# Two layers of a hybrid encoder on one core: a sixth load buffer, copies of the norms split over two engines, and block-sum steps moved inside the matmul pairs

## The chip, the core and the metric

The kernel runs on one core of a Trainium2 chip. Five engines work side by side, each through its own queue in order: TensorE (PE, matmuls into PSUM; its weight loads are shown as PEld), VectorE (DVE), ScalarE (ACT), GpSimd (POOL) and SyncE (SP, which issues the transfers here). They wait for each other through semaphores. The metric is the device time of one execution in microseconds (us); lower is better.

## The reference, cut to what matters

The input is 256 tokens of 2048 features in float32. There are two layers. Each does `x = x + mixer(rmsnorm(x))` and then `x = x + swiglu(rmsnorm(x))`; the mixer is grouped attention in layer 0 and a gated recurrent block in layer 1. The change concerns the feed-forward half and the norms that feed it and the next mixer:

```python
def rms_norm(x, g):
    y = xf * lax.rsqrt(jnp.mean(xf * xf, axis=-1, keepdims=True) + EPS)
    return (y * g.astype(jnp.float32)).astype(x.dtype)

def swiglu(h, w_gate, w_up, w_down):        # D = 2048, D_FF = 5632
    return (jax.nn.silu(h @ w_gate) * (h @ w_up)) @ w_down

for i in range(DEPTH):                      # DEPTH = 2
    ...
    x = x + mix
    x = x + swiglu(rms_norm(x, norm_ffn[i]), w_gate[i], w_up[i], w_down[i])
```

## The kernel before, in words

**Precision.** Every weight and activation is split into a rounded part "hi" and a remainder "lo". A product is three matmuls (hi·hi, hi·lo, lo·hi) into one float32 accumulator of 512 columns.

**Loads.** Weights come as halves of 512 KB, 128 x 1024 numbers. `load_half` issues one transfer from SP's queue into a `raw` buffer (L111), casts it on ScalarE into `hi` (L120) and subtracts on VectorE into `lo` (L121). There are five `raw`, five `hi` and five `lo` buffers, used in turn. So a transfer waits until the half five places earlier was cast and subtracted, and a cast waits until TensorE is done with the half five places earlier. The order of the halves (`order`, `ffn_order`) is written out by hand and must be the order in which TensorE uses them.

**Pairs.** The feed-forward part goes in parts of 12, 16 and 16 hidden tiles (`PARTS`). For each four hidden tiles a "unit" multiplies the normalised tokens with 512 columns of w_gate and of w_up at the same time; this is one call of `project_pair`, with eight steps over the 16 feature tiles. After a part's units, `down` multiplies the part's hidden tiles with w_down in two such pairs (columns 0-1 and 2-3 of four), with six steps in the part of 12 and eight in the parts of 16. A pair has four accumulators, `banks[j][a]` with j the half of the columns and a the half of the tokens, in the four PSUM buffers of `new_acc`. The next pair uses the same four, in the order [0][0], [0][1], [1][0], [1][1], and its first products wait until VectorE has taken the old contents out.

**Steps.** A usual step takes two halves and eight products (24 matmuls, L275). In two steps of each pair, those named in `SEVEN`, a block scheme does the same with seven products (21 matmuls). It needs sums of the weight blocks: VectorE makes `wx` with four additions once both halves have landed (L245 to L248; L246 also rewrites the second `raw` before its cast), ScalarE casts `wxh` (L252), and VectorE subtracts `wxl` (L253). The fifth to seventh product read them; the first four do not. The sums of the token blocks are made by `x_forms`. The partial results go to four more PSUM banks, and once the second such step is done `merge` puts them together: a copy on ScalarE (L311) that can start after the step's first product, and four additions on VectorE (L312 to L315). Then VectorE adds the accumulators: in a unit onto gate and up (L755, L758), in `down` first four additions of the merged results onto the residual stream `x_tok` (L489), then the four accumulators (L498).

**After a unit** come SiLU on ScalarE (L515), the product with up (L759), and `turned`: two 32 x 32 transposes on VectorE (L440) into a single buffer `tb`, and 16 copies of 32 x 256 on ScalarE (L445) into a single buffer `tf`, then the hi and lo of four hidden tiles (L764, L765).

**Norms.** `Norm.add` is called for each 512 columns of `x_tok` that are final: two squares on ScalarE (L404), `turned`, and the hi and lo of four feature tiles (L396, L397). So the last columns of a mixer are turned while the first pair of the feed-forward part is running. The recurrent block begins with `project_two`, which uses the first eight feature tiles for two outputs, then four more, then the last four.

**Who sets the order.** TensorE's order is the order of the program. On the other engines a scheduler orders the instructions when the program is built, from its own estimate of times; on the chip each engine keeps that order.

Of the kernel before, what the change touches and what calls it, by code (L numbers as in the profile page):

```python
# [12 lines left out]
F32 = mybir.dt.float32  # L13
# [5 lines left out]
P = 128  # L19
S = 256  # L20
D = 2048
KT = D // P
# [4 lines left out]
DFF = 5632  # L27
PARTS = [12, 16, 16]
SEVEN = {6: (1, 3), 8: (2, 5)}
HALF = 8  # L30
WIDE = 512
NCOL = D // WIDE
FOUR = WIDE // P
# [37 lines left out]
def trunk(ctx, tc, w, out):  # L71
    nc = tc.nc
    act, dve, pool, pe, sync = nc.scalar, nc.vector, nc.gpsimd, nc.tensor, nc.sync

    cst = ctx.enter_context(tc.tile_pool(name="cst", bufs=1))
    wp = ctx.enter_context(tc.tile_pool(name="wp", bufs=3))
# [10 lines left out]
    def nm(s):  # L87
        uid[0] += 1
        return f"{s}_{uid[0]}"
# [15 lines left out]


    def load_half(src, n, pieces=1, then=None, before=None):
        raw = wp.tile([P, HALF, P], F32, tag="raw", name=nm("raw"), bufs=5)
        hi = wp.tile([P, HALF, P], F32R, tag="hi", name=nm("hi"), bufs=5)
        lo = wp.tile([P, HALF, P], F32R, tag="lo", name=nm("lo"), bufs=5)  # L110
        newest["load"] = sync.dma_start(out=raw[:, :n, :], in_=src[:, :n, :])  # L111
        newest["raw"] = raw
        if then:
            then()
        if before:
            before(raw)
        for i in range(pieces):
            sl = slice(i * n // pieces, (i + 1) * n // pieces)
            newest["tiles"] = hi, lo
            newest["cast"] = act.copy(hi[:, sl, :], raw[:, sl, :])  # L120
            dve.tensor_tensor(lo[:, sl, :], raw[:, sl, :], hi[:, sl, :].bitcast(F32), ALU.subtract)  # L121
        return [(hi[:, i, :], lo[:, i, :]) for i in range(n)]


    def halves(src, kt):
        return [(src[:, a : min(a + HALF, kt), :], min(HALF, kt - a)) for a in range(0, kt, HALF)]

    def wide(name):
        src = w[name]
        return [(src[c, i], HALF) for c in range(src.shape[0]) for i in range(src.shape[1])]  # L130

    def ffn_order(l):
        units = [wide(f"w_gate{l}"), wide(f"w_up{l}")]
        seq, i = [], 0
        for p, n in enumerate(PARTS):
            for _ in range(n // FOUR):
                seq += sum(zip(*(u[i : i + KT // 2] for u in units)), ())
                i += KT // 2
            down = wide(f"w_down{l}_{p}")
            for c in range(0, len(down), n):  # L140
                seq += sum(zip(down[c : c + n // 2], down[c + n // 2 : c + n]), ())
        return seq

    order = [(w["w_k"][i], HALF) for i in range(len(KEY_TILES))]
    order += sum((halves(w["w_qv"][h % 20], KT) for h in range(NQ, NQ + 20)), [])
    order += wide("w_o") + ffn_order(0)
    for b in range(-1, NBLK):
        xin = range(2 * b + 2, 2 * b + 4) if b + 1 < NBLK else []
        yin = range(KT + 2 * b, KT + 2 * b + 2) if b >= 0 else []
        both = [halves(w["w_in"][c], KT) for c in (*xin, *yin)]  # L150
# [35 lines left out]
    def step():  # L186
        clock[0] += 1
        due = [i for i, (t, _) in enumerate(waiting) if t <= clock[0]]
        if due:
            waiting.pop(due[0])[1]()  # L190
# [5 lines left out]
    def new_acc():  # L196
        return ps_a.tile([P, 2 * S], F32, tag="acc", name=nm("acc"))
# [37 lines left out]
    def flat(t):  # L235
        return t.rearrange("p (k c) f -> p k (c f)", k=2)
# [29 lines left out]
        dve.tensor_tensor(t[:, 1], y[:, 4:, :], t[:, 0].bitcast(F32), ALU.subtract)  # L266
        return [(t[:, 0, i, :], t[:, 1, i, :]) for i in range(4)]

    def project_pair(xs, forms, middle):
        banks = [[new_acc() for _ in range(2)] for _ in range(2)]  # L270
        begun = set()

        def product(acc, x, wt, last=False):
            for i, (a, b) in enumerate(((x[0], wt[0]), (x[0], wt[1]), (x[1], wt[0]))):
                pe.matmul(acc, a, b, start=id(acc) not in begun, stop=last and i == 2)  # L275
                begun.add(id(acc))
            step()
            step()

        def tokens(k, a):  # L280
            return [xs[k][:, o + a * P : o + (a + 1) * P] for o in (0, S)]

        end = len(xs) // 2 - 1
        for n in range(end + 1):
            if n in forms:
                s1, s2, s3, s4 = forms[n]
                b11, b21, t3, b22, t1, t2, t4 = seven_forms()
                if n == min(forms):
                    p1, q6, q5, q7 = (ps_m.tile([P, WIDE], F32, tag="pm", name=nm("pm")) for _ in range(4))
                last = n == max(forms)  # L290
                product(p1, tokens(2 * n, 0), b11, last)
                product(banks[0][0], tokens(2 * n + 1, 0), b21)
                product(banks[1][0], s4, b22)
                product(q7, s3, t3, last)
                product(q5, s1, t1, last)
                product(q6, s2, t2, last)
                product(banks[0][1], tokens(2 * n + 1, 1), t4)
                if last:
                    middle(p1, q5, q6, q7)
            else:  # L300
                for j in range(2):
                    half()
                    hi, lo = (flat(t) for t in newest["tiles"])
                    for a in range(2):
                        for k in range(2):
                            product(banks[j][a], tokens(2 * n + k, a), (hi[:, k, :], lo[:, k, :]), n == end and k == 1)
        return banks

    def merge(p1, q5, q6, q7):
        g, u = (fp[0].tile([P, 2, WIDE], F32, tag=t, name=nm(t), bufs=1) for t in ("fg", "fu"))  # L310
        act.copy(g[:, 0, :], p1)  # L311
        dve.tensor_tensor(g[:, 1, :], q6, g[:, 0, :], ALU.subtract)  # L312
        dve.tensor_tensor(u[:, 0, :], q5, g[:, 1, :], ALU.add)
        dve.tensor_tensor(g[:, 1, :], q7, g[:, 1, :], ALU.subtract)
        dve.tensor_tensor(u[:, 1, :], u[:, 0, :], q7, ALU.subtract)  # L315
        return g, u
# [66 lines left out]
    class Norm:  # L383
# [18 lines left out]
        def add(self, c):  # L402
            for a in range(2):
                act.activation(tmp("nj", (P, WIDE), bufs=1), x_tok[:, a, c, :], AF.Square, accum_out=self.sums[:, a, c : c + 1])  # L404
            for f in turned(x_tok[:, :, c, :]):
                self.operand(f, True)
            for n in SEVEN[KT // 2] if self.seven else ():
                if FOUR * c <= 2 * n < FOUR * c + FOUR:
# [24 lines left out]

    def turned(src):
        b = fp[0].tile([P, 2, FOUR, P], F32, tag="tb", name=nm("tb"))
        f = fp[0].tile([P, 8, FOUR, 32], F32, tag="tf", name=nm("tf"))
        for a in range(2):
            dve.transpose(b[:, a, :, :], src[:, a, :])  # L440
        for q in range(4):
            for i in range(4):
                o, y = f[32 * i : 32 * i + 32, q::4, :, :], b[32 * q : 32 * q + 32, :, i, :]
                y = y.rearrange("p a (k t) -> p a k t", k=FOUR)
                act.copy(o, y)  # L445
        return [f[:, :, k, :] for k in range(FOUR)]

    fp = []
# [65 lines left out]
    def table_act(*a, **k):  # L514
        table_op(act.activation(*a, **k))  # L515
# [194 lines left out]
    def act_tile():  # L710
        return xp.tile([P, 2 * S], F32R, tag="act", name=nm("act"), bufs=18)
# [35 lines left out]


    def ffn(norm, nxt):
        def unit(hid, forms, seven):  # L750
            got = []
            banks = project_pair(norm.xs, norm.forms, lambda *banks: got.extend(merge(*banks)))
            g, u = got
            for a, acc in enumerate(banks[0]):
                dve.tensor_tensor(g[:, a, :], acc, g[:, a, :], ALU.add)  # L755
                table_act(g[:, a, :], g[:, a, :], AF.Silu, scale=norm.rt[:, a : a + 1])
            for a, acc in enumerate(banks[1]):
                dve.tensor_tensor(u[:, a, :], acc, u[:, a, :], ALU.add)  # L758
                dve.scalar_tensor_tensor(u[:, a, :], u[:, a, :], norm.rt[:, a : a + 1], g[:, a, :], ALU.mult, ALU.mult)  # L759
            first = len(hid)  # L760
            for f in turned(u):
                h = act_tile()
                hi, lo = (h[:, o : o + S].rearrange("p (q t) -> p q t", t=32) for o in (0, S))
                act.copy(hi, f)  # L764
                dve.tensor_tensor(lo, f, hi.bitcast(F32), ALU.subtract)  # L765
                hid.append(h)
            for i, n in enumerate(seven):
                if first <= 2 * n < len(hid):
                    forms[n] = x_forms(hid[2 * n], hid[2 * n + 1], f"hf{i}")

        for p, n in enumerate(PARTS):
            hid, forms = [], {}
            for _ in range(n // FOUR):
                unit(hid, forms, SEVEN[n // 2])
            last = p == len(PARTS) - 1
            if last and nxt is not None:
                ln_exp_tables()
            down(hid, forms, nxt if last else None, last and nxt is None)
# [106 lines left out]
    units = [(d, j) for j in range(2) for d in range(2)]  # L885
# [114 lines left out]
```

## Time and profile before

| | |
|---|---|
| time, median of three runs | 2037.86 us (2032.6 to 2040.56) |
| profiled execution: its time, and the span on the core | 2037.47 us, 2035.7 us |
| TensorE busy | 1996.2 us, 98% |
| VectorE busy | 1692.5 us, 83% |
| ScalarE busy | 1369.3 us, 67% |
| GpSimd busy | 168.7 us, 8% |
| granted TensorE clock, mean | 0.992 |
| traffic | 386 MB, 190 GB/s; 57% of the transfer engines' span |

A row of a timeline gives the start and the duration in us, then engine, line, operation, and `out<-in` by the names of tiles; an `x4` merges four like instructions; the bracket at the end is the idle time before it and what ended it. The matmuls are pipelined: each is shown with 0.39 us though one starts every 0.227 us, so starts are compared and not durations. On VectorE and ScalarE, too, one instruction starts shortly before the row of the last one ends. A row of the windows view gives the borders of a stretch and its length, then busy time and number of instructions of PE, PEld, DVE, ACT and POOL, then the granted clock, the share of the transfer engines, and GB/s.

### The profile page before, as it was taken

The numbers are of one execution on the slowest core, as the hardware profiler recorded it, in microseconds if no ns is written. First come the engines' busy times: TensorE is split into PE (matmuls) and PEld (weight loads), VectorE is DVE, ScalarE is ACT, GpSimd is POOL, SyncE is SP. The second block draws the span as 40 slices with busy tenths as digits, with TensorE's granted clock in tenths as the row PEclk, the third lists the DMA queues.
The fourth block names the chain that finished last, engine by engine and source line by source line (L and its number), as shares of the span: only waits on it lengthen the run. The fifth ranks groups of instructions, "written<-read, shape, count | busy, mean of one in ns | idle before, by whom it ended". The sixth has DMA issues, their size and how long they took to land.

```text
span 2035.7 us, 27908 instructions
## 1 busy us (share of the span) xinstructions
PE 1996.2 (98%) x9920; PEld 1689.5 (83%) x9920; DVE 1692.5 (83%) x2351; ACT 1369.3 (67%) x2166; POOL 168.7 (8%) x213
## 2 busy tenths in 40 slices
PE   9999999999999999999799999999999999999999
PEld 8898878878888888887699998878788878888887
DVE  8998678987888888888679887688897888878887
ACT  7665876664667446677789988767745766457663
POOL 1563000000000000000133330000000000000000
PEclk9999999999999999999899999999999999999999
DMA  8444555556555665655456554656556556655564
GB/s 320 156 135 145 194 180 194 188 191 196 191 201 183 222 197 189 205 184 196 155 172 187 184 176 158 207 167 205 186 188 195 188 199 213 196 193 187 199 217 145
DMA packets 109003, 386.06 MB, mean 190 GB/s; under 512 B 12224, under 2 KB 12992, under 8 KB 108736
## 3 DMA queue, kind: packets, MB, share of 16 engines
q1 hardware_dynamic: 108720, 384.26, 57.1%
q8 instruction: 78, 1.28, 0.2%
q14 instruction: 61, 0.50, 0.1%
q10 hardware_dynamic: 144, 0.02, 0.0%
HBM read 382.13 MB, written 2.10 MB: 189 GB/s over the span
## 4 chain that ended last, share of the span: by engine, by line
PE 47%; issue 42%; DVE 7%; DMA 2%; ACT 2%; POOL 0%; SPq 0%; DVEq 0%; ACTq 0%; POOLq 0%
PE acc L275 23%; PE acc L228 4%; PE acc L206 4%; PE pm L275 3%; DVE lo L121 3%; PE acc L319 3%; PE acc L320 3%; PE acc L321 3%; PE pm L320 1%; PE pm L321 1%; PE pm L319 1%; DMA raw<-in_w_up_dram 1%; ACT tf L445 1%; ACT hi L120 1%; DMA raw<-in_w_down_dram 0%
## 5 line engine op out<-in xcount | busy, mean ns | idle before, releaser
L120 ACT CAST hi<-raw 128x1024 fp32r<-128x1024 f32 (+1 forms) x708 | 727.6, 1045 | 477.6 <-PE acc L275 372.1
L121 DVE TENSOR_TENSOR lo<-raw,hi 128x1024 fp32r<-128x1024 f32 (+1 forms) x708 | 852.4, 1223 | 135.3 <-ACT hi L120 133.9
L275 PE MATMUL acc<-hi,xg 128*128 128x512 f32 x2200 | 697.7, 390 | 3.0 <-DVE fg L755 2.9
L275 PEld LDWEIGHTS acc<-hi,xg 128*128 128x128 f32 x2200 | 413.8, 188 | 95.5 <-issue 6.4
L275 PE MATMUL acc<-lo,xg 128*128 128x512 f32 x1100 | 428.6, 390 | 0.0
L275 PE MATMUL acc<-hi,act 128*128 128x512 f32 x1072 | 342.6, 391 | 0.9 <-DVE fg L755 0.7
L275 PEld LDWEIGHTS acc<-lo,xg 128*128 128x128 f32 x1100 | 207.0, 188 | 42.3
L275 PEld LDWEIGHTS acc<-hi,act 128*128 128x128 f32 x1072 | 201.9, 188 | 48.4 <-issue 3.0
L445 ACT COPY tf<-tb 32x256 f32<-32x256 f32 x544 | 219.5, 404 | 9.2 <-DVE xg L397 1.0
L275 PE MATMUL acc<-lo,act 128*128 128x512 f32 x536 | 209.2, 390 | 0.0
L228 PE MATMUL acc<-hi,act 128*128 128x512 f32 x512 | 159.9, 390 | 0.0
L319 PE MATMUL acc<-xg,hi 128*128 128x256 f32 x512 | 147.0, 287 | 11.7 <-ACT xg L396 11.7
L320 PE MATMUL acc<-xg,hi 128*128 128x256 f32 x512 | 146.6, 286 | 0.5 <-DVE xg L397 0.5
L245 DVE TENSOR_TENSOR wx<-raw,raw 128x512 f32<-128x512 f32 x68 | 47.0, 691 | 119.7 <-DMA raw<-in_w_up_dram 91.5
L321 PE MATMUL acc<-xg,lo 128*128 128x256 f32 x512 | 146.0, 285 | 0.0
L253 DVE TENSOR_TENSOR wxl<-wx,wxh 128x1536 fp32r<-128x1536 f32 x68 | 119.1, 1752 | 22.4 <-ACT wxh L252 22.1
L206 PE MATMUL acc<-xg,hi 128*128 128x512 f32 x384 | 125.7, 396 | 0.2 <-ACT hi L120 0.2
L252 ACT CAST wxh<-wx 128x1536 fp32r<-128x1536 f32 x68 | 100.3, 1476 | 34.5 <-DVE wx L248 34.5
L275 PEld LDWEIGHTS acc<-lo,act 128*128 128x128 f32 x536 | 100.9, 188 | 20.4
L228 PEld LDWEIGHTS acc<-hi,act 128*128 128x128 f32 x512 | 96.1, 188 | 19.6
L319 PEld LDWEIGHTS acc<-xg,hi 128*128 128x128 f32 x512 | 99.8, 195 | 12.1 <-ACT xg L396 12.1
L320 PEld LDWEIGHTS acc<-xg,hi 128*128 128x128 f32 x512 | 99.7, 195 | 1.1 <-DVE xg L397 1.0
(238 smaller groups left out, 2830.4 us busy)
## 6 DMA issues: line engine op xcount, KB each, us to landing
raw<-in_w_gate_dram SPq DMA_DIRECT2D x176, 512.0 KB, 4.4
raw<-in_w_up_dram SPq DMA_DIRECT2D x176, 512.0 KB, 4.3
raw<-in_w_down_dram SPq DMA_DIRECT2D x176, 512.0 KB, 4.3
raw<-in_w_in_dram SPq DMA_DIRECT2D x64, 512.0 KB, 4.5
raw<-in_w_qv_dram SPq DMA_DIRECT2D x40, 512.0 KB, 4.3
raw<-in_w_o_dram SPq DMA_DIRECT2D x32, 512.0 KB, 3.6
raw<-in_w_out_dram SPq DMA_DIRECT2D x32, 512.0 KB, 4.3
graw<-in_w_gates_dram SPq DMA_DIRECT2D x32, 256.0 KB, 3.5
```

Source lines behind the costliest of these rows:

```text
L120: newest["cast"] = act.copy(hi[:, sl, :], raw[:, sl, :])
L121: dve.tensor_tensor(lo[:, sl, :], raw[:, sl, :], hi[:, sl, :].bitcast(F32), ALU.subtract)
L206: pe.matmul(o, w, x, start=(k == 0 and not part), stop=(k == total - 1 and not part))
L228: pe.matmul(accs[a], x, wt[:, k, :], start=(k0 + k == 0 and n == 0), stop=(end and k == 1 and n == 2))
L245: dve.tensor_tensor(x[:, 0, :], r2[:, 0, :], r1[:, 0, :], ALU.add)
L252: act.copy(xh, x)
L253: dve.tensor_tensor(xl, x, xh[:].bitcast(F32), ALU.subtract)
L275: pe.matmul(acc, a, b, start=id(acc) not in begun, stop=last and i == 2)
L319: pe.matmul(o, hi, x[:, :S], start=start, stop=False)
L320: pe.matmul(o, hi, x[:, S:], start=False, stop=False)
L321: pe.matmul(o, lo, x[:, :S], start=False, stop=stop)
L445: act.copy(o, y)
```

## The change

Three edits. `raw` has six buffers in place of five. In the norms (not in the units) every second of the 16 copies of `turned` goes to VectorE. And the steps of a pair are taken in a listed order: in the first pair of each layer's feed-forward part 0, 1, 3, 4, 2, 6, 5, 7, so that the block-sum steps (2 and 5) come fifth and seventh and no longer third and sixth; in the pairs of six 0, 2, 1, 4, 3, 5, so that the block-sum steps (1 and 3) come third and fifth and no longer second and fourth. Other pairs of eight stay as they are. The halves are loaded in the new order.

```diff
+USUAL_STEPS = {6: (0, 2, 1, 4, 3, 5), 8: (0, 1, 2, 3, 4, 5, 6, 7)}
+FIRST_STEPS = (0, 1, 3, 4, 2, 6, 5, 7)
...
-        raw = wp.tile([P, HALF, P], F32, tag="raw", name=nm("raw"), bufs=5)
+        raw = wp.tile([P, HALF, P], F32, tag="raw", name=nm("raw"), bufs=6)
...
+    def pair_steps(n, first=False):
+        return FIRST_STEPS if first else USUAL_STEPS[n]
...
             for _ in range(n // FOUR):
-                seq += sum(zip(*(u[i : i + KT // 2] for u in units)), ())
+                for k in pair_steps(KT // 2, i == 0):
+                    seq += [u[i + k] for u in units]
                 i += KT // 2
             down = wide(f"w_down{l}_{p}")
             for c in range(0, len(down), n):
-                seq += sum(zip(down[c : c + n // 2], down[c + n // 2 : c + n]), ())
+                for k in pair_steps(n // 2):
+                    seq += [down[c + k], down[c + n // 2 + k]]
...
-        end = len(xs) // 2 - 1
-        for n in range(end + 1):
+        steps = pair_steps(len(xs) // 2, first)
+        seven = [n for n in steps if n in forms]
+        for n in steps:
             if n in forms:
...
-                if n == min(forms):
+                if n == seven[0]:
...
-                last = n == max(forms)
+                last = n == seven[-1]
...
-                            product(banks[j][a], tokens(2 * n + k, a), (hi[:, k, :], lo[:, k, :]), n == end and k == 1)
+                            product(banks[j][a], tokens(2 * n + k, a), (hi[:, k, :], lo[:, k, :]), n == steps[-1] and k == 1)
...
-    def turned(src):
+    def turned(src, both=True):
...
-                act.copy(o, y)
+                if i % 2 and both:
+                    dve.tensor_copy(o, y)
+                else:
+                    act.copy(o, y)
...
-            for f in turned(u):
+            for f in turned(u, False):
...
-            for _ in range(n // FOUR):
-                unit(hid, forms, SEVEN[n // 2])
+            for i in range(n // FOUR):
+                unit(hid, forms, SEVEN[n // 2], p == i == 0)
```

More of the change, by code (lines that the diff above doesn't have):

```diff
@@ L267, in x_forms, with project_pair @@
         return [(t[:, 0, i, :], t[:, 1, i, :]) for i in range(4)]
-    def project_pair(xs, forms, middle):
+    def project_pair(xs, forms, middle, first=False):
         banks = [[new_acc() for _ in range(2)] for _ in range(2)]
@@ L749, in ffn, with unit @@
     def ffn(norm, nxt):
-        def unit(hid, forms, seven):
+        def unit(hid, forms, seven, first):
             got = []
-            banks = project_pair(norm.xs, norm.forms, lambda *banks: got.extend(merge(*banks)))
+            banks = project_pair(norm.xs, norm.forms, lambda *banks: got.extend(merge(*banks)), first)
             g, u = got
```

## The prediction, made before the changed kernel was run

> **What bounds the kernel now.** I read the page first, then the waits, the windows of single pairs, and the timelines around each stop.
>
> ```profile
> PE 1996.2 (98%) x9920; PEld 1689.5 (83%) x9920; DVE 1692.5 (83%) x2351; ACT 1369.3 (67%) x2166; POOL 168.7 (8%) x213
> ```
>
> TensorE is the bound, so the change can win only what TensorE stands still or runs slowly, and lose by making it stop elsewhere. The waits view names who stops whom (total, times, longest):
>
> ```profile
> PE pm L275 <- ACT wxh L252: 6.3, 4, 2.0
> PE pm L275 <- DVE wxl L253: 6.2, 5, 1.3
> PE acc L275 <- DVE fg L755: 3.6, 6, 1.4
> ACT hi L120 <- PE acc L275: 372.1, 210, 5.0
> DVE wx L245 <- DMA raw<-in_w_up_dram: 91.5, 37, 4.0
> ```
>
> The first two rows are the weight sums of a few block-sum steps that come late. The windows, cut where a pair's first matmul starts, say which (layer 0: first pair, first and second down pair of six, an undisturbed pair of eight; layer 1: first pair, first down pair of six):
>
> ```profile
> 267.45:314.54 47.09, 44.59 (x187) 35.89 (x186) 38.18 (x52) 31.20 (x48) 0.00 (x0) 0.96 0.57 190
> 399.63:436.40 36.77, 33.56 (x139) 26.83 (x138) 31.68 (x41) 23.18 (x37) 0.00 (x0) 0.95 0.53 171
> 436.40:468.14 31.74, 31.73 (x139) 25.75 (x138) 31.02 (x37) 15.58 (x15) 0.00 (x0) 1.00 0.65 215
> 468.14:510.30 42.16, 42.16 (x187) 34.91 (x186) 32.03 (x36) 20.68 (x21) 0.00 (x0) 1.00 0.60 188
> 1318.74:1365.81 47.07, 44.58 (x188) 35.91 (x186) 38.51 (x52) 31.21 (x48) 0.00 (x0) 0.96 0.57 191
> 1451.19:1489.62 38.43, 35.02 (x139) 27.81 (x139) 31.96 (x41) 23.43 (x37) 0.00 (x0) 0.91 0.51 164
> ```
>
> A matmul every 0.227 us gives 5.44 us for a usual step (24) and 4.76 for a block-sum step (21): 42.16 for eight steps, 31.28 for six. So each first pair loses 4.9 us, the first down pair of six 5.0 and 6.7, the second only 0.5. VectorE is busy 31.0 of 31.74 us in the second: it has no slack there. One such stop, on TensorE:
>
> ```profile
> 418.00 0.39 PE L275 MATMUL pm<-hi,hf 128*128 128x512 f32 x1
> 420.31 0.50 PE L275 MATMUL pm<-wxh,hf 128*128 128x512 f32 x1 [1.91 <-ACT wxh L252]
> 422.10 0.79 PE L275 MATMUL pm<-wxl,hf 128*128 128x512 f32 x1 [1.29 <-DVE wxl L253]
> ...
> 424.40 0.63 PE L275 MATMUL acc<-wxh,act 128*128 128x512 f32 x1
> 424.82 0.62 PE L275 MATMUL acc<-wxl,act 128*128 128x512 f32 x1
> 425.75 0.39 PE L275 MATMUL acc<-lo,act 128*128 128x512 f32 x1
> ```
>
> From 418.00 to 425.75 eleven matmuls start, which need 2.50 us: 5.25 lost, 3.20 of it idle, 2.05 at half pace (424.40 to 424.82 is 0.42). A stop costs its idle time and some 2.05 us more.
>
> **Part A, first pairs (block-sum steps fifth and seventh): -5.0 us.** The late `wxh` stands on ScalarE behind the 16 copies of the norm's last columns. At the fifth place it is wanted 10.9 us later (two usual steps), and the copies ahead of it are halved; the 2 x 4.9 us go. What is late next: `merge` now has one step before the pair ends instead of two. Call E the end of the last block-sum step; TensorE wants the second accumulator emptied at E + (24+6) x 0.227 = E+6.8. VectorE's order in the changed program (no times in it) puts there w1 lo w2 lo M1 w3 M2 A1 w4 M3 M4 lo A2, with w the weight sums of the next pair, M the merge, A the accumulators. With the starts of these rows, 0.60 us for a 512-column addition and 1.13 for a subtraction of a half, this is 10 x 0.60 + 3 x 1.13 = 9.4 us:
>
> ```profile
> 450.77 1.75 DVE L253 TENSOR_TENSOR wxl<-wx,wxh 128x1536 fp32r<-128x1536 f32 x1
> 452.44 2.58 DVE L121 TENSOR_TENSOR lo<-raw,hi 128x1024 fp32r<-128x1024 f32 x2
> ...
> 464.00 1.22 DVE L121 TENSOR_TENSOR lo<-raw,hi 128x1024 fp32r<-128x1024 f32 x1
> 465.13 0.68 DVE L498 TENSOR_TENSOR x_tok<-x_tok,acc 128x512 f32<-128x512 f32 x1
> 465.73 0.69 DVE L246 TENSOR_TENSOR raw<-raw 128x512 f32<-128x512 f32 x1
> ```
>
> w1 waits for a load that is issued when the half six places earlier is subtracted. That half's cast waits until TensorE is done with the half five before it, at E-4.76-2.72 = E-7.5; with the cast, the subtraction and the transfer it lands at E-7.5 + 1.05 + 1.13 + 4.3 = E-1.0:
>
> ```profile
> L120 ACT CAST hi<-raw 128x1024 fp32r<-128x1024 f32 (+1 forms) x708 | 727.6, 1045 | 477.6 <-PE acc L275 372.1
> raw<-in_w_down_dram SPq DMA_DIRECT2D x176, 512.0 KB, 4.3
> ```
>
> So A2 ends at E+8.4: 1.6 us late. I take 2.4, with part of a slow stretch; bounds 0 and 1.6 + 2.05. Net per layer -2.5, bounds -4.9 and -1.2.
>
> What a stop costs beside its idle time hangs on the clock. The Trainium skill (TensorE: Matmul & The Clock Gate, "What's actually happening") halves the clock only after an idle window of about 3.4 us. By that rule the two gaps of 1.91 and 1.29 us would cost 3.2 us, not 5.25; this trace contradicts it, and the rows decide.
>
> **Part B, pairs of six (third and fifth).** *Within the first down pair: 0.* Its late `wxh` gets one step more, but step 4 moves up to the fourth place, and it reads the last unit's hidden tiles:
>
> ```profile
> 411.18 6.63 ACT L445 COPY tf<-tb 32x256 f32<-32x256 f32 x16
> 421.11 1.32 ACT L764 CAST act<-tf 128x256 fp32r<-128x256 f32 x4
> 423.10 1.43 DVE L765 TENSOR_TENSOR act<-tf,act 128x256 fp32r<-128x256 f32 x4
> ```
>
> They are wanted at 15.6 us after the pair's start (2 x 5.44 + 4.76); now they come at 21.5 and 23.5. These copies stay on ScalarE, in the changed order behind the cast of the second step's second half, which waits until TensorE is done with the half five earlier (8.2 us), and ahead of three casts: 9.2 + 6.6 + 3 x 1.0 = 18.8, hi of the first tile at 19.2, its lo after one subtraction at 20.4, wanted at 16.1. A stop of 4.3 + 2.05 = 6.3 us, against 5.25 and 6.7 before: no change, bounds -2 and +4 for the two layers.
>
> *At the end of both down pairs: +32.1 us.* In `down` the merge is followed by four additions onto `x_tok` before the accumulators, and there is again one step for it. The order on VectorE is X w1 lo w2 lo M1 w3 A1 M2 w4 lo M3 M4 X wxl X X lo A3 w1 A2: 16 x 0.60 + 4 x 1.13 + 1.67 = 15.8 us (15.2 after the second pair, without the last w1). It begins when the copy of the first product is there, not before E - 18 x 0.227 + 0.6 = E-3.5:
>
> ```profile
> L311 ACT COPY fg<-pm 128x512 f32<-128x512 f32 x34 | 19.5, 575 | 0.0
> ```
>
> So A2 ends at E+12.3 (E+11.7 after the second pair), or up to 2.1 us later where the cast ahead of the copy and the load that w1 wants (landing about E-1.0, as above) hold it up; TensorE wants it at E+6.8. A stop of 4.9 to 7.6 us; I take 6.2, with 2.05 for the clock, four times: 33.0, less the 2 x 0.46 that the second pairs lose now. The least it can be follows from the buffers: the last lo ahead of A2 needs a cast that waits for the pair's last matmul, so A2 is not done before 1.05 + 1.13 + 2 x 0.60 = 3.4 us after the pair, wanted at 1.4: 2.0 us, +7.1 in all. The most: 4 x (7.6 + 4.1) - 0.9 = +46.
>
> **Part C, norm copies on two engines: -9.3 us.** Between the layers TensorE waits for two batches, one after the other because `tb` and `tf` are single:
>
> ```profile
> 992.89 0.58 PE L319 MATMUL acc<-xg,hi 128*128 128x256 f32 x1 [8.39 <-ACT xg L396]
> 1002.34 0.58 PE L319 MATMUL acc<-xg,hi 128*128 128x256 f32 x1 [3.26 <-ACT xg L396]
> 985.61 6.60 ACT L445 COPY tf<-tb 32x256 f32<-32x256 f32 x16
> 995.14 6.61 ACT L445 COPY tf<-tb 32x256 f32<-32x256 f32 x16 [1.01 <-DVE xg L397]
> 992.24 1.31 DVE L440 STREAM_TRANSPOSE tb<-x_tok 128x512 f32<-128x512 f32 x2 [5.13 <-ACT tf L445]
> L356 DVE CAST qs<-hq 128x256 fp32r<-128x256 f32 x16 | 4.6, 288 | 0.4 <-POOL hq L588 0.4
> ```
>
> Eight copies take ScalarE 3.3 us. A copy of 32 x 256 on VectorE isn't in the trace; from below it is bounded by nothing better than half the cast of 256 columns on 128 partitions, 0.15, from above by ScalarE's own 0.41. I take the cast's 0.29, the nearest row: eight are 2.3 us, hidden beside ScalarE's 3.3. Two batches save 6.6, and the first stands one square and one cast earlier on ScalarE: 1.4. That is -8.0, bounds -4 (VectorE's subtractions hold the second batch) and -10 (a slow stretch goes too). In layer 0's last down pair the same batches make a `wxl` late, 1.3 us with its restart, which goes (bounds -1.3 and 0):
>
> ```profile
> 965.71 0.50 PE L275 MATMUL pm<-wxl,hf 128*128 128x512 f32 x1 [1.01 <-DVE wxl L253]
> 1649.53 0.47 PE L275 MATMUL acc<-hi,xg 128*128 128x512 f32 x1 [1.36 <-DVE fg L755]
> ```
>
> **Part D, six raw buffers: -3 us.** SP's queue issues each load one half (2.72 us) sooner, so VectorE waits less for loads (91.5 us over 37 waits, 2.5 each) and empties accumulators sooner at other pair ends, as in the row at 1649.53. There the whole is 3.6 us idle, some 4.7 with restarts; bounds -4.7 and +2. The transfer engines have room (share 0.5 to 0.65).
>
> **Sum**, against the profiled execution's 2037.47 (the median is 0.4 higher): -5.0 + 0 + 32.1 - 9.3 - 3.0 = +14.8, 2052 us.
>
> **The rivals.**
> 1. *The accumulators come only as late as the buffers force, 2.0 us, with no slow stretch, and the gains stand.* For it: the scheduler interleaves, and gaps such as 1.36 us pass without a slow stretch. Against it: VectorE's 31.0 of 31.74 us. Price: +7.1 in place of +32.1, 2027.3. It decides if VectorE reaches A2 within 3.4 us of the pair's end. Chance 0.20.
> 2. *Long stops slow the clock twice,* as the wait of 8.39 us might. 4 x 2.05 more, and the hidden tiles 4 more: 2064. Chance 0.13.
> 3. *The gain between the layers is taken back:* the recurrent block's gates wait for a chain on VectorE that now also has copies. Then -8.0 becomes -2: 2058. Chance 0.12.
>
> **How the numbers follow.** My forecast has 0.55, and its own range is 2041 to 2062. The likeliest time is 2052. The range that leaves out no more than 2 in 10 reaches into the first two rivals: 2031 to 2066. What a measurement tells from no change is about 0.5%, 2027.7 to 2048.0. Half of rival 1 lies below (0.10); its other half and 0.13 of my forecast lie within (0.23); the rest is slower (0.67).
>
> **What would show it.** Windows of the four down pairs of six and the pair after each: stops of 5 to 7.6 us ahead of a first product, named after VectorE's L509; none means that Part B is wrong and rival 1 or better holds. First pairs: 42 to 43 us, then a stop of some 2 us on L766. Fourth step of the first down pair: a wait for the hidden tiles (L775, L776) in place of `wxh`. Between the layers: 16 copies as two eights of 3.3 us, and the second batch's stop gone. If the hidden tiles or the accumulators come in time, the prediction is wrong by their terms.

## The result, and the profile after

| | before | changed |
|---|---|---|
| median (lowest to highest, 4 runs each) | 2036.48 us (2032.6 to 2040.56) | 2050.36 us (2050.14 to 2052.43) |
| ratio, with its 95% interval | | 1.0063 (1.0045 to 1.0081) |
| profiled execution: time, span | 2037.47, 2035.7 us | 2050.14, 2048.1 us |
| mean granted clock | 0.992 | 0.986 |

The changed kernel is slower by 0.63%. Its line numbers have moved: the matmuls of the steps are L282, the casts and subtractions of the loads L122 and L123, the weight sums L252 to L255, `wxh` L259, `wxl` L260, the merge L319 to L323, the additions onto `x_tok` L500 (merged) and L509 (accumulators), in a unit L766 and L769, the norm copies L454 (VectorE) and L456 (ScalarE), the hidden tiles L775 and L776.

First the waits of the changed kernel (total, times, longest):

```profile
PE acc L282 <- DVE x_tok L509: 23.7, 4, 6.2
PE acc L282 <- ACT act L775: 8.4, 2, 4.3
PE acc L282 <- DVE act L776: 0.9, 2, 0.4
PE acc L327 <- ACT xg L404: 3.5, 1, 3.5
PE acc L282 <- DVE fg L766: 2.9, 3, 1.3
DVE wx L252 <- DMA raw<-in_w_up_dram: 32.7, 33, 2.2
```

The weight sums are no longer among TensorE's main stops. In their place stand four waits of 5.9 us on average for the accumulators of `down`, and two of 4.2 us for the hidden tiles. VectorE's wait for loads of w_up fell from 91.5 to 32.7 us.

The windows of layer 0, cut at the first matmuls of the first pair, the second pair, the two down pairs of six, and the pair after them:

```profile
268.18:310.34 42.16, 42.16 (x187) 34.91 (x186) 36.93 (x54) 27.68 (x39) 0.00 (x0) 1.00 0.63 198
310.34:354.59 44.25, 42.62 (x187) 34.67 (x186) 38.17 (x51) 29.06 (x43) 0.00 (x0) 1.00 0.54 176
397.09:435.73 38.64, 34.08 (x139) 27.28 (x138) 30.50 (x38) 24.04 (x38) 0.00 (x0) 0.91 0.55 174
435.73:474.62 38.89, 33.15 (x139) 26.98 (x138) 29.89 (x35) 15.73 (x16) 0.00 (x0) 0.91 0.53 162
474.62:525.45 50.83, 44.91 (x187) 36.60 (x186) 37.48 (x42) 21.50 (x21) 0.00 (x0) 0.93 0.52 168
```

The first pair takes the undisturbed 42.16 us, where it took 47.09. The stretch of the pair after it is 2.1 us longer, 1.6 of it at that pair's own start. The first down pair of six takes 7.4 us more than its 31.28 (5.5 before), the second 7.6 (0.5 before), and the pair after them 8.7 us more than 42.16 (none before).

One of the four end stops, on TensorE and then on VectorE:

```profile
436.87 0.39 PE L282 MATMUL acc<-hi,act 128*128 128x512 f32 x1
443.00 0.79 PE L282 MATMUL acc<-hi,act 128*128 128x512 f32 x1 [5.74 <-DVE x_tok L509]
```

```profile
433.52 0.68 DVE L509 TENSOR_TENSOR x_tok<-x_tok,acc 128x512 f32<-128x512 f32 x1
434.12 0.69 DVE L321 TENSOR_TENSOR fu<-pm,fg 128x512 f32<-128x512 f32 x1
434.72 0.68 DVE L255 TENSOR_TENSOR wx<-wx,raw 128x512 f32<-128x512 f32 x1
...
437.65 0.69 DVE L500 TENSOR_TENSOR x_tok<-x_tok,fu 128x512 f32<-128x512 f32 x1
438.25 1.75 DVE L260 TENSOR_TENSOR wxl<-wx,wxh 128x1536 fp32r<-128x1536 f32 x1
439.92 0.69 DVE L500 TENSOR_TENSOR x_tok<-x_tok,fg 128x512 f32<-128x512 f32 x1
440.52 0.69 DVE L500 TENSOR_TENSOR x_tok<-x_tok,fu 128x512 f32<-128x512 f32 x1
441.12 1.22 DVE L123 TENSOR_TENSOR lo<-raw,hi 128x1024 fp32r<-128x1024 f32 x1
442.26 0.68 DVE L509 TENSOR_TENSOR x_tok<-x_tok,acc 128x512 f32<-128x512 f32 x1
```

VectorE has no gap in these rows. TensorE's first product into the new accumulator starts 0.74 us after the start of the addition that empties it; between the first and the next L509 stand three additions of the merge, three onto `x_tok`, two subtractions of halves, one weight sum and `wxl`.

The hidden tiles in the first down pair, on ScalarE and TensorE:

```profile
407.04 6.65 ACT L456 COPY tf<-tb 32x256 f32<-32x256 f32 x16 [0.49 <-DVE tb L448]
413.71 2.94 ACT L122 CAST hi<-raw 128x1024 fp32r<-128x1024 f32 x3
416.56 1.32 ACT L775 CAST act<-tf 128x256 fp32r<-128x256 f32 x4
```

```profile
417.01 0.80 PE L282 MATMUL acc<-hi,act 128*128 128x512 f32 x1 [4.11 <-ACT act L775]
```

Between the layers, the copies as two eights on two engines, and the one stop that is left:

```profile
994.20 2.38 DVE L454 COPY tf<-tb 32x256 f32<-32x256 f32 x8
994.42 3.30 ACT L456 COPY tf<-tb 32x256 f32<-32x256 f32 x8
999.87 0.58 PE L327 MATMUL acc<-xg,hi 128*128 128x256 f32 x1 [3.45 <-ACT xg L404]
L454 DVE COPY tf<-tb 32x256 f32<-32x256 f32 x96 | 27.4, 285 | 1.5
```

These rows are from the timelines, the last from the groups. For the whole span I added up TensorE's losses by place: the time from one matmul's start to the next, less what it takes at full pace (0.227 us at 512 columns). "Middle" is the third and fourth place of the first down pairs, "ends" the first steps after the four down pairs of six; each column is both layers together.

| us lost | first pairs | pair after | middle | ends | between layers | whole span |
|---|---|---|---|---|---|---|
| before | 9.8 | 0 | 11.9 | 0.9 | 16.9 | 63.5 |
| changed | 0 | 3.1 | 15.4 | 33.0 | 7.7 | 76.8 |

The difference is 13.3; the spans differ by 12.4. By place it is -6.7 (first pairs and the pairs after), +3.5, +32.1, -9.2, and a remainder of -6.4, most of it at other pair ends.

### The profile page after: what moved, and what is told of

It is laid out like the page before. It is cut to its first block, busy times and chain, and to the rows that moved or that the text cites. A ratio compares the mean times of both kernels' runs of the same rounds, so it can differ in the third digit from the quotient of the medians.

```text
span 2048.1 us, 27927 instructions
## 1 busy us (share of the span) xinstructions
PE 1996.1 (97%) x9920; PEld 1694.8 (83%) x9920; DVE 1725.7 (84%) x2447; ACT 1336.5 (65%) x2070; POOL 167.6 (8%) x213
## 4 chain that ended last, share of the span: by engine, by line
PE 81%; DVE 10%; issue 3%; DMA 3%; ACT 3%; POOL 0%; SPq 0%; DVEq 0%; ACTq 0%; POOLq 0%
PE acc L282 50%; PE acc L235 8%; PE pm L282 7%; DVE lo L123 4%; PE acc L213 3%; PE acc L328 3%; PE acc L327 3%; PE acc L329 3%; ACT tf L456 1%; PE pm L328 1%; PE pm L329 1%; PE pm L327 1%; ACT hi L122 1%; DMA raw<-in_w_down_dram 1%; DMA x<-in_x_dram 1%
## 5 line engine op out<-in xcount | busy, mean ns | idle before, releaser
L122 ACT CAST hi<-raw 128x1024 fp32r<-128x1024 f32 (+1 forms) x708 | 731.5, 1047 | 559.8 <-PE acc L282 408.1
L123 DVE TENSOR_TENSOR lo<-raw,hi 128x1024 fp32r<-128x1024 f32 (+1 forms) x708 | 858.3, 1226 | 211.5 <-ACT hi L122 209.1
L282 PE MATMUL acc<-hi,xg 128*128 128x512 f32 x2200 | 698.5, 391 | 14.7 <-DVE x_tok L509 11.7
L282 PEld LDWEIGHTS acc<-hi,xg 128*128 128x128 f32 x2200 | 415.4, 189 | 105.0 <-DVE x_tok L509 12.6
L282 PE MATMUL acc<-lo,xg 128*128 128x512 f32 x1100 | 429.9, 391 | 0.0
L282 PE MATMUL acc<-hi,act 128*128 128x512 f32 x1072 | 346.0, 396 | 21.2 <-DVE x_tok L509 11.9
L282 PEld LDWEIGHTS acc<-hi,act 128*128 128x128 f32 x1072 | 204.8, 191 | 67.5 <-DVE x_tok L509 12.8
L282 PEld LDWEIGHTS acc<-lo,xg 128*128 128x128 f32 x1100 | 207.7, 189 | 43.1
L282 PE MATMUL acc<-lo,act 128*128 128x512 f32 x536 | 211.6, 395 | 0.0
L456 ACT COPY tf<-tb 32x256 f32<-32x256 f32 x448 | 181.2, 404 | 8.7 <-DVE tb L448 2.5
L260 DVE TENSOR_TENSOR wxl<-wx,wxh 128x1536 fp32r<-128x1536 f32 x68 | 119.2, 1753 | 9.8 <-ACT wxh L259 9.7
L282 PEld LDWEIGHTS acc<-lo,act 128*128 128x128 f32 x536 | 102.8, 192 | 21.3
L259 ACT CAST wxh<-wx 128x1536 fp32r<-128x1536 f32 x68 | 100.7, 1481 | 25.8 <-DVE wx L255 17.0
L329 PEld LDWEIGHTS acc<-xg,lo 128*128 128x128 f32 x512 | 99.6, 195 | 0.0
```

The source lines that it names most:

```text
L259: act.copy(xh, x)
L260: dve.tensor_tensor(xl, x, xh[:].bitcast(F32), ALU.subtract)
L329: pe.matmul(o, lo, x[:, :S], start=False, stop=stop)
```

## The experiments

All are edits of the changed kernel, so they have its line numbers; only where the accumulators are added first do the later lines move on (the additions onto `x_tok` are then L506 for merged results and L515 for accumulators, the hidden tiles L783 and L784). A ratio is against runs of the kernel before on the same chip in the same set, whose median was 2036 to 2040 us; sets are compared by ratio. The losses by place:

| us lost | first pairs | pair after | middle | ends | between layers | whole span |
|---|---|---|---|---|---|---|
| only the pairs of six moved | 11.0 | 0 | 14.6 | 15.5 | 17.5 | 84.3 |
| changed, five raw buffers | 0 | 1.7 | 15.2 | 16.2 | 7.6 | 67.1 |
| changed, old order in the pairs of six | 0 | 3.1 | 8.1 | 2.7 | 7.7 | 41.9 |
| changed, accumulators first | 0 | 3.1 | 15.1 | 2.0 | 7.7 | 45.0 |
| changed, last unit's copies split | 0 | 3.1 | 7.0 | 30.0 | 7.7 | 65.4 |
| only the norm copies | 0.2 | 0.6 | 11.7 | 0.9 | 7.7 | 50.4 |
| only six raw buffers | 0 | 0.4 | 8.0 | 2.7 | 15.9 | 47.6 |
| only the first pairs moved | 0 | 3.3 | 4.9 | 3.0 | 17.2 | 51.3 |
| both old orders, six raw, norm copies | 0 | 0 | 6.7 | 4.0 | 7.7 | 33.6 |
| changed, both covers | 0 | 3.0 | 7.2 | 2.1 | 7.7 | 34.8 |
| both old orders, both covers | 0 | 0 | 11.0 | 1.8 | 7.7 | 37.0 |
| first pairs moved, both covers | 0 | 3.1 | 11.1 | 0.8 | 7.6 | 39.1 |

### Is it the pairs of six?

The first kernel undoes the move in the pairs of six and keeps the rest:

```diff
-USUAL_STEPS = {6: (0, 2, 1, 4, 3, 5), 8: (0, 1, 2, 3, 4, 5, 6, 7)}
+USUAL_STEPS = {6: (0, 1, 2, 3, 4, 5), 8: (0, 1, 2, 3, 4, 5, 6, 7)}
```

> The changed kernel with the pairs of six back in the steps' old order (block-sum steps second and fourth); the other edits stay. Theory (the moved steps of the pairs of six make the stops): the four stops at the pair ends (7.6, 8.7, 8.1 and 8.6 us by the starts of the matmuls) go back to some 0.9 in all, and the two stops inside the first down pairs (7.4 and 8.1) to what they were before (5.2 and 6.7): 2050.4 - 32 - 3.5, about 2015 us. Rival (six raw buffers let the scheduler put more of the next pair's sums ahead of the accumulators, whatever the steps' order): stops of 3 us or more stay at the four pair ends, 2025 us or more.

Measured: 2013.0 us, ratio 0.9885 (0.987 to 0.9899). The move in the pairs of six alone turns a gain of 1.15% into a loss of 0.63%: 37 us, of which the table shows 30 at the ends and 7 in the middle. The ends keep 2.7 us, where the theory had 0.9, and the middle falls below that of the kernel before (8.1 for 11.9).

The second makes this move alone:

```diff
-FIRST_STEPS = (0, 1, 3, 4, 2, 6, 5, 7)
+FIRST_STEPS = (0, 1, 2, 3, 4, 5, 6, 7)
...
-        raw = wp.tile([P, HALF, P], F32, tag="raw", name=nm("raw"), bufs=6)
+        raw = wp.tile([P, HALF, P], F32, tag="raw", name=nm("raw"), bufs=5)
...
-    def turned(src, both=True):
+    def turned(src, both=False):
```

> The kernel before with one edit alone, the pairs of six in the new order. Theory: the stops at the pair ends do not need the sixth buffer, and cost about 32 us, with some 3.5 more inside the first down pairs: 2036.5 + 35, about 2072 us. Rival (the sixth buffer is needed for the stops): less than half of it, 2054 us or less.

Measured: 2057.11 us, ratio 1.0095 (1.008 to 1.0111). It falls between the theory and its rival, because the ends lost 15.5 us and not 33. So the size of the end stops hangs on another part of the change. The next kernel asks which: the changed kernel with five raw buffers.

```diff
-        raw = wp.tile([P, HALF, P], F32, tag="raw", name=nm("raw"), bufs=6)
+        raw = wp.tile([P, HALF, P], F32, tag="raw", name=nm("raw"), bufs=5)
```

> The changed kernel with five raw buffers again. With the pairs of six alone moved (the run e2) the four stops at the pair ends were 15.4 us in all, in the changed kernel 33.0. Theory (the sixth buffer doubles them, because the next pair's sums stand ahead of the accumulators): the stops fall to some 15.4 us, and the 8 us at the other pair ends come back: 2050.4 - 17.6 + 8, about 2041 us. Rival (the copies or the first pairs' order lengthen the stops, not the buffer): stops of 30 us or more stay, 2055 us or more.

Measured: 2041.55 us, ratio 1.001 (1.0 to 1.0021), with 16.2 us lost at the ends. It is the sixth raw buffer that doubles the end stops. VectorE and TensorE of this kernel at the end of the same pair, which lies 0.67 us earlier here (435.06 for 435.73):

```profile
432.53 0.68 DVE L321 TENSOR_TENSOR fu<-pm,fg 128x512 f32<-128x512 f32 x1
...
437.87 0.68 DVE L500 TENSOR_TENSOR x_tok<-x_tok,fu 128x512 f32<-128x512 f32 x1
438.47 0.68 DVE L509 TENSOR_TENSOR x_tok<-x_tok,acc 128x512 f32<-128x512 f32 x1
...
442.42 1.76 DVE L260 TENSOR_TENSOR wxl<-wx,wxh 128x1536 fp32r<-128x1536 f32 x1 [0.34 <-ACT wxh L259]
```

```profile
439.20 0.50 PE L282 MATMUL acc<-hi,act 128*128 128x512 f32 x1 [2.62 <-DVE x_tok L509]
```

With five buffers the next pair's `wxl` stands behind all four accumulators' additions; with six it stands ahead of the last three, as the changed kernel's rows show (438.25), and the merge's second addition (L321) comes at 434.12 for 432.53. From the pair's end TensorE's product comes after 4.1 us here (439.20 less 435.06) and after 7.3 in the changed kernel (443.00 less 435.73). The rows show the order; that earlier loads led the scheduler to it is the likely reason, and was not tested by itself.

### Which work makes the two stops

In the pairs of six, the accumulators are added to `x_tok` ahead of the merged results (the same eight additions):

```diff
             def middle(*banks):
-                g, u = merge(*banks)
-                for j, t in enumerate((g, u)):
+                merged[:] = merge(*banks)
+                if len(xs) != PARTS[0]:
+                    add_merged()
...
+            if len(xs) == PARTS[0]:
+                add_merged()
```

> The changed kernel, but in the pairs of six VectorE adds the four accumulators onto x_tok before the four merged results instead of after them; same sums, other order. Theory (a queue of VectorE work that stands ahead of the accumulators makes the stop): A2 then stands right behind the second merge addition, about E+5, and TensorE wants it at E+6.8: the four stops go to 0 to 1 us each, 2050.4 - 31, about 2019 us. Rival (the buffers of hi and lo force 2.0 us or more, or the restart of the clock stays): 2 to 4 us stay at each of the four ends, 2027 us or more.

Measured: 2019.38 us, ratio 0.9914 (0.9899 to 0.9928). The ends fall from 33.0 to 2.0 us with the same instructions on VectorE in another order; the middle stays. VectorE and TensorE at the end of the same pair, whose last matmul is followed by the next pair's first at 434.49:

```profile
432.80 0.68 DVE L515 TENSOR_TENSOR x_tok<-x_tok,acc 128x512 f32<-128x512 f32 x1
433.40 0.68 DVE L321 TENSOR_TENSOR fu<-pm,fg 128x512 f32<-128x512 f32 x1
434.00 0.68 DVE L515 TENSOR_TENSOR x_tok<-x_tok,acc 128x512 f32<-128x512 f32 x1
```

```profile
437.76 0.47 PE L282 MATMUL acc<-hi,act 128*128 128x512 f32 x1 [0.39 <-DVE x_tok L515]
```

The second accumulator's addition now stands one place behind the first's, and is over before TensorE wants it. The third makes TensorE wait 0.39 us. The end stops are thus the merged results and the next pair's sums ahead of the accumulators, not a shortage of VectorE as such.

The last unit's hidden tiles copied on both engines:

```diff
-            for f in turned(u, False):
+            for f in turned(u, both):
...
-                unit(hid, forms, SEVEN[n // 2], p == i == 0)
+                unit(hid, forms, SEVEN[n // 2], p == i == 0, i == n // FOUR - 1)
```

> The changed kernel, and in the last unit of each part every second of the 16 copies of 32 x 256 goes to VectorE too. Theory (the step moved to the fourth place waits for the last unit's hidden tiles behind those 16 copies on ScalarE): the tiles come 3.3 us sooner, the two stops of 7.4 and 8.1 us shrink to 1 to 4 us: 2050.4 - 10, about 2040 us. Rival (the casts ahead of the tiles, which wait for TensorE to free their buffers, set them): less than 2 us in all, 2048 us or more.

Measured: 2037.07 us, ratio 1.0001 (0.9991 to 1.001). The middle falls from 15.4 to 7.0 us, the ends stay at 30. The copies on ScalarE are what makes the hidden tiles' hi late in the changed order. What is left is a wait for their lo on VectorE (L776), 2.1 and 2.2 us in the two layers.

Both edits together:

> The changed kernel, with the four accumulators of a pair of six added to x_tok ahead of the four merged results, and with the last unit's hidden tiles copied on both engines. Theory: the ends of the pairs of six (32.97 us in the changed kernel, 1.8 with the additions turned round) and the stops on the hidden tiles (15.4 us, 7.0 with the copies on both engines) are separate terms and add up: -31 and -8, so 2050 - 39 = 2011 us, ratio 0.987. Rival: VectorE has no time for both, the copies push the accumulators back: the ends lose 10 us or more, 2020 or above, ratio 0.992 or above.

Measured: 2008.4 us, ratio 0.9858 (0.9841 to 0.9874). The two add up (middle 7.2, ends 2.1).

### What each other part brings alone

The norm copies alone, the six raw buffers alone, and the moved first pairs alone, each with the other three edits undone.

> The kernel before with one edit alone, the norms' copies on both engines. Theory (Part C): the waits between the layers fall from 16.9 to some 8 us by the matmuls' starts, and nothing else changes: 2036.1 - 9, 2027 us. Rival (the halved copies also free the weight sums that come late in the first pairs, so that their 2 x 4.6 us go without any moved step): 2018 us.

> The kernel before with one edit alone, six raw buffers. The changed kernel lost some 8 us less at the ends of the pairs whose steps did not move. Theory (VectorE waits less for loads and empties the accumulators sooner): this comes from the sixth buffer alone, 2036.1 - 8, 2028 us. Rival (it comes from the moved steps or the copies): 2033 us or more.

> The kernel before with one edit alone, the first pairs' block-sum steps fifth and seventh. Theory (Part A): the stops of 4.6 us in the two first pairs go, and a stop of 1.6 us comes at the end of each: 2036.1 - 6, 2030 us. Rival (without the halved copies the stop only moves, to another step that waits for the last columns' tiles): within 2 us of before.

Measured: 0.9931 (0.9915 to 0.9946), 0.9906 (0.9889 to 0.9923) and 0.9934 (0.9917 to 0.9951), which is 14, 19 and 13 us on 2037. Each theory had less: 9, 8 and 6 us. The table says why: every one of the three takes away the whole stop of the first pairs, 9.8 us, which the prediction had given to the moved steps alone. ScalarE in layer 0's first pair, before, with only the norm copies, with only six raw buffers, one fence each:

```profile
274.38 6.65 ACT L445 COPY tf<-tb 32x256 f32<-32x256 f32 x16
281.05 0.20 ACT L515 ACTIVATE rsq_s<-nrt 128x2 f32<-128x2 f32 x1
281.16 1.46 ACT L252 CAST wxh<-wx 128x1536 fp32r<-128x1536 f32 x1
```

```profile
268.53 1.49 ACT L259 CAST wxh<-wx 128x1536 fp32r<-128x1536 f32 x1 [2.35 <-DVE wx L255]
...
273.74 3.31 ACT L456 COPY tf<-tb 32x256 f32<-32x256 f32 x8 [0.47 <-DVE tb L448]
```

```profile
273.23 1.49 ACT L259 CAST wxh<-wx 128x1536 fp32r<-128x1536 f32 x1
...
276.25 6.64 ACT L456 COPY tf<-tb 32x256 f32<-32x256 f32 x16 [0.59 <-DVE nrt L423]
```

In both, the cast of `wxh` stands ahead of the norm's copies, where before it stood behind them. The sixteen copies with only six raw buffers still take 6.64 us, and TensorE loses nothing in that pair.

The norm copies alone stand between their theory and its rival: the first stop goes too, but some 6 us come back in small stops at other places. The single gains don't add up (46 us), since the first stop is in all three. Which leaves the question whether the moved first pair is of any use: both orders undone, six raw buffers and the norm copies kept.

```diff
-USUAL_STEPS = {6: (0, 2, 1, 4, 3, 5), 8: (0, 1, 2, 3, 4, 5, 6, 7)}
-FIRST_STEPS = (0, 1, 3, 4, 2, 6, 5, 7)
+USUAL_STEPS = {6: (0, 1, 2, 3, 4, 5), 8: (0, 1, 2, 3, 4, 5, 6, 7)}
+FIRST_STEPS = (0, 1, 2, 3, 4, 5, 6, 7)
```

> Six raw buffers and the norms' copies on both engines stay; both orders of steps are those of before. Theory A: the stop of the first pair (2 x 4.9 us before) needs no moved step, since it is gone with either of the two other parts alone; the moved first pair then only brings the late accumulator after it (1.58 and 1.47 us beside the old order of the pairs of six), so this runs 3 us shorter than that kernel's 2013 us: 2010, ratio 0.987. Theory B (each part has a gain of its own, as predicted): the first pair's stop comes back, at least half of it, 5 us or more: 2015 or above, ratio 0.9895 or above.

Measured: 2007.26 us, ratio 0.9853 (0.9838 to 0.9867): theory A. The page's first line, and the windows of the same places (first pair, both down pairs of six, the pair after them):

```profile
PE 1982.2 (99%) x9920; PEld 1686.1 (84%) x9920; DVE 1723.4 (86%) x2447; ACT 1334.3 (67%) x2070; POOL 168.3 (8%) x213
```

```profile
267.25:309.41 42.16, 42.16 (x187) 34.92 (x186) 38.22 (x54) 27.28 (x39) 0.00 (x0) 1.00 0.64 210
393.73:427.79 34.06, 32.09 (x140) 25.60 (x138) 30.69 (x39) 23.06 (x38) 0.00 (x0) 1.00 0.56 186
427.79:461.72 33.93, 31.93 (x138) 25.82 (x139) 31.74 (x38) 15.85 (x15) 0.00 (x0) 1.00 0.57 189
461.72:503.90 42.18, 42.18 (x188) 34.92 (x187) 33.28 (x36) 21.61 (x21) 0.00 (x0) 1.00 0.63 208
```

VectorE is busy as long as in the changed kernel (1723.4 for 1725.7 us) and TensorE's stops have gone. The first pair needs no moved step. Against the kernel with the first pairs moved and the old pairs of six (0.9885) this is 0.0032 less, some 6.5 us: 3.1 of it is the stop in the pair after, which the moved block-sum steps bring; the rest is spread over the middle (8.1 for 6.7) and small stops, and was not followed up. This is the best version of the study, together with the changed kernel with both covers: the two can't be told apart by their intervals.

The two covers on top of the old orders, and the same with the first pairs moved:

> As the kernel with both old orders, six raw buffers and the norms' copies on both engines, with the last unit's hidden tiles copied on both engines and the accumulators of a pair of six added ahead of the merged results. Theory: the stops in the middle of the first down pair of six (4.0 us each with five usual copies) and at the ends of the pairs of six (1.3 us each) are what is left; the additions turned round take the ends (-2.6), the copies perhaps half of the middle (-4): 2003 to 2006 us, ratio 0.984. Rival: in the old order the middle stop is on the weight sum and not on the hidden tiles, so VectorE's part of the copies makes it later: no better than the old orders alone, 2010 to 2014, ratio 0.987 or above.

> As the kernel before it in this set, with the first pair's block-sum steps fifth and seventh. Theory A: the moved first pair costs the late accumulator after it and gains nothing: 3 us more than with the old order, some 2006 to 2009 us, ratio 0.0015 above the other's. Theory B: the moved first pair still wins its stop: at least 5 us less than with the old order.

Measured: 2010.83 us, ratio 0.987 (0.9856 to 0.9885), and 2013.11 us, 0.988 (0.9865 to 0.9894). The first met its rival: the ends lose a little less (1.8 for 4.0 us) but the middle more (11.0 for 6.7), since there the late thing is a weight sum, and VectorE now has copies and hidden tiles ahead of it. VectorE and TensorE of this kernel in the middle of the first down pair:

```profile
412.22 1.43 DVE L784 TENSOR_TENSOR act<-tf,act 128x256 fp32r<-128x256 f32 x4
413.56 1.22 DVE L123 TENSOR_TENSOR lo<-raw,hi 128x1024 fp32r<-128x1024 f32 x1
414.69 1.75 DVE L260 TENSOR_TENSOR wxl<-wx,wxh 128x1536 fp32r<-128x1536 f32 x1
```

```profile
416.50 0.50 PE L282 MATMUL pm<-wxl,hf 128*128 128x512 f32 x1 [2.89 <-DVE wxl L260]
```

Where the hidden tiles come behind `wxl` (only both old orders), this wait is 1.30 us. The ratio's interval overlaps with that of the old orders alone, so the harm is read from the middle's losses and not from the time. The covers that take 8 us from the middle of the changed order add 4 to the old one. The second kernel's losses show the moved first pairs' 3.1 us once more, and no gain; the two ratios' intervals overlap.

## Why the prediction was right, point by point

- **Part A, first pairs, -5.0: measured -6.7.** The stop of 4.9 us a layer went, and the second accumulator's wait of 1.6 us came, 1.61 and 1.53 us, on L766 as foreseen. The term was mis-sized by the part of a slow stretch that was added (2.4 taken): 1.6 us alone slows nothing here. But that the move is what wins it falls: with the sixth buffer or the split copies beside it, the stop goes without the move (the kernel with both old orders), and the move then costs.
- **Part B, middle of the first down pair, 0: measured +3.5.** The stop did move from `wxh` to the hidden tiles, behind the 16 copies and three casts. The first hi was foreseen 19.2 us after the pair's start and starts at 19.5 (416.56 less 397.09). The idle part is 4.1 to 4.3 us, foreseen 4.3; what was short is the slow stretch and the second gap for the lo: 7.35 and 8.08 us in all for 6.3. Within the bounds of -2 and +4.
- **Part B, ends, +32.1: measured +32.1.** Four stops of 5.9 us idle and 2.3 for the clock stand against 6.2 and 2.05: the two misses cancel, so the exact sum is luck; the mechanism is not. The merged results' additions onto `x_tok`, the next pair's sums and `wxl` stand ahead of the awaited accumulator in the order that the prediction wrote down; the awaited accumulator is the one just ahead of the last weight sum, one place of 0.60 us sooner than was taken; the kernel with the accumulators first shows that this order is the cause. The changed program's own order was needed for this: by the order with five buffers the stops would have been half as large.
- **Part C, norm copies, -9.3: -9.2 between the layers, where -8.0 was foreseen, and -0.25 in the last down pair for -1.3.** That the sum fits is again two misses that cancel. A copy on VectorE takes 285 ns, where 0.29 was taken from the cast. The batches are 3.3 us, and the second stop is gone. In the last down pair 1.04 us are still lost to `wxl`, for 1.29.
- **Part D, six raw buffers, -3.0: a remainder of -6.4 at the other pair ends and elsewhere**, beyond the lower bound of -4.7. The mechanism stands (VectorE's wait for loads of w_up is 32.7 us for 91.5), the size was too small. The remainder, which is the whole span less the table's five places, shows whose this gain is: 24.0 us before, 20.6 with only six raw buffers, 29.3 with only the norm copies, 26.4 in the changed kernel with five raw buffers, 17.6 with six. So the sixth buffer takes 3.4 us alone and 8.8 in the changed kernel, and the copies put some 5 back. Alone the part brings 19 us, because it also takes the first pairs' stop, and 4 us of the middle.
- **The sum, +14.8, stands against +12.7 of the profiled executions.** Its largest term was exact; those of A and D were too small in gain, B's middle too small in loss, and these misses partly cancel.
- **The rivals.** The accumulators came 5.9 us late and not 2.0, so the first falls. Long stops did slow the clock for two windows, as the second says, but part of the two windows passes while TensorE stands: 2.3 us a stop and not 4.1. The third falls: the stretch of the gates behind the norm lost 7.0 us for 6.5, not the 6 us more.

With only the first pairs moved, the middle lost 4.9 us for 11.9. The timelines show how: in layer 0 ScalarE begins the 16 copies 10.3 us after the pair's start for 11.5, TensorE's wait for `wxh` is 0.56 us for 1.91, and no half-pace stretch follows. What stays open is why the scheduler's order gives ScalarE this lead there, and at which places the norm copies alone give back some 6 us of their two gains (9.6 and 9.2, with 13.1 seen in the whole span).

## What to carry to other kernels

When several edits each take away the same stop, their single gains are not to be added: test each part in the company of the others, and drop the one that then only costs. Where two steps share accumulators, what counts at a pair's end is the place of the emptying additions in the busy engine's queue, not its busy share; putting them first was worth 31 us without one instruction less. Here, a cover that moved work to another engine helped where that engine's next product wasn't the late one (8 us less in the middle), and cost where it was (4 us more).

## What the runs showed of the hardware

The granted clock goes by fixed windows. All half-pace stretches in these traces begin on a grid of 3.41 us and last one or more of its steps (3.41, 6.83 and 10.24 us are the usual lengths; the last of each trace is cut off by its end). The same two waits of 0.6 and 1.30 us fell differently on this grid in the two layers of the kernel with both old orders. Its windows view, cut on the grid (PE's busy time is the second number; the granted clock the third from the end):

```profile
409.87:413.28 3.41, 2.86 (x12) 1.88 (x10) 1.64 (x2) 3.37 (x6) 0.00 (x0) 1.00 0.72 269
413.28:416.69 3.41, 2.11 (x10) 1.67 (x10) 3.41 (x6) 3.41 (x7) 0.00 (x0) 1.00 0.41 157
1444.10:1447.51 3.41, 1.54 (x6) 0.88 (x6) 3.26 (x5) 3.41 (x8) 0.00 (x0) 1.00 0.55 181
1447.51:1450.92 3.41, 3.41 (x10) 2.65 (x9) 3.41 (x7) 1.89 (x2) 0.00 (x0) 0.50 0.19 55
```

In layer 0 a border lies between the waits, and no window is granted half; in layer 1 both lie in one window, 1.87 us idle together, and the next runs ten matmuls at half pace. The two waits cost 2.4 us in layer 0 and 4.0 in layer 1. Over the traces of all fourteen kernels, after the first 260 us, a full-pace window with 1.77 us idle or more was followed by a half-pace one every time (66 of 66), one with 0.9 to 1.55 never (0 of 49), and between these both occur (4 of 12). So two short waits can bring a half-pace window if they share a window of the grid, as one longer wait does. The stop of 1.6 us after the changed kernel's first pairs, 1.31 and 1.24 us of it idle, brought none. And differences of some 2 us between these kernels can come from where a wait falls on the grid.

The Trainium skill (TensorE: Matmul & The Clock Gate, "What's actually happening") has the free-running window of 3413 ns, and the traces agree. Its condition of an idle window for the slower state doesn't hold here: about half a window idle was enough.
